# First down step of each expert chunk run one chunk later, with its weights loaded one chunk later

## The chip, the core and the metric

The kernel runs on one core of a Trainium2 chip. The metric is the device time of one execution in microseconds. Engines are named as the profile names them: PE is the matrix engine (its queue is PEq), DVE and ACT the vector and the scalar engine, POOL and SP the two others; SP issues nearly all transfers.

## The reference

A two-layer decoder trunk on 256 tokens of width 1024 in float32. What matters here is its last large part, a mixture of experts:

```python
logits = (xn @ router).astype(jnp.float32)
top_vals, top_idx = lax.top_k(logits, TOP_K)
...
for e in range(N_EXPERTS):
    out = out + combine[..., e:e + 1].astype(xn.dtype) * swiglu(xn, wg[e], wu[e], wd[e])
```

`swiglu` is `(silu(x @ wg) * (x @ wu)) @ wd`. There are 8 experts, each token goes to two of them, and the hidden width of an expert is 3584. All weights of all experts are read: 8 x 3 x 1024 x 3584 float32 numbers, 352 MB of the 447 MB that the program moves.

## The kernel before, in words

**Chunks.** The hidden width of an expert is cut into 7 chunks of 512 columns, so there are 56 chunks in `order`, numbered 0 to 55 here (chunks 0 to 6 are expert 0, 7 to 13 expert 1, and so on). A chunk has six weight tiles of 1 MB (128 x 2048 float32): two of gate, two of up, two of down.

**Slots.** The tokens of an expert are gathered into slots. The first 64 slots are always computed. Two further groups of 32 slots follow under `where_more`, which puts the work in a `tc.If` on the expert's count: more than 64 tokens opens group 0, more than 96 opens group 1 also. PE branches on that count.

**One pass of the loop (index i)** records, in this order:
1. `gate_up(i)`: 16 matmuls for the first 64 slots. The 64 output columns of the array's left half hold gate, those of the right half hold up, so two matmuls run side by side.
2. `hidden(i)`: silu and product on ACT and DVE. Then one piece of background work: a `gather` of the next expert's tokens (in an expert's last two chunks) or a `scatter` of a finished expert.
3. `where_more`: for the further groups, `down_b` of chunk i-2, transposes `turn_b` of chunk i-1, and `gate_up_b` of chunk i. `down_b` and `gate_up_b` use strips of 32 columns, so four matmuls run side by side.
4. `give_back`: the four gate and up tiles of chunk i and the two down tiles of chunk i-2 go back to the free list, and each is refilled at once by the next load of the stream (`Stream.load`, on SP, which waits until the tile's last reader is done).
5. `down` of chunk i-1 for the first 64 slots: 8 matmuls, `n` = 0 in the left half, `n` = 1 in the right half.
6. `turned_a(i)`: four transposes of the hidden values, copied by DVE to `hTa` for the next pass's `down`.

`with behind()` keeps the order of the first-slot steps on PE. What stands around them on an engine is set by the recording layer, not by the source alone.

**Loads.** The whole tiles are loaded in the order in which `add_whole` names them: gate and up of chunk i, then down of chunk i-1. There are 19 tile buffers in the pool at this stage. A down tile is read by `down` in one pass and by `down_b` in the next.

The functions and the loop follow, with the line numbers of the profile. In the profile of this kernel L1064 is `gate_up`, L1131 `down`, L1138 `down_b`, L1086 `gate_up_b`, L1113 the transposes of `turned_a`, L1121 those of `turn_b`, L994 `gather`, L1165 `scatter`, L1186 and L1189 the two branches of `where_more`, and L134 the loads on SP. One float32 matmul leaves two records.

Of the kernel before, what the change touches and what calls it, by code (L numbers as in the profile page):

```python
# [22 lines left out]
NT = T // P  # L23
# [13 lines left out]
NE, ED = 8, 3584  # L37
EC = ED // 512
# [178 lines left out]
def build(nc, tc, ctx, a, out):  # L217
# [15 lines left out]
    S = Stream(nc)  # L233

    def add_tiles(w, n):

        per, m = w.shape[2] // n, PS // n
        for t in range(w.shape[0]):
            S.add(w[t], [min(m, per - i) for i in range(0, per, m)], n)

    w = a["w_down_q"]
# [8 lines left out]
    t = 0  # L250
# [7 lines left out]
            add_tiles(a[w][g], 384)  # L258
    add_tiles(a["dsw_wo"], D)
    order = [(e, c) for e in range(NE) for c in range(EC)]  # L260
    for i, (e, c) in enumerate(order):
        if not i:
            add_tiles(a["moe_gate"][e, c], 512)
        for t in range(2):
            for nm in ("moe_gate", "moe_up")[not i:]:
                S.add_whole(a[nm][e, c][t])
        for t in range(2 if i else 0):
            S.add_whole(a["moe_down"][order[i - 1]][t])
    for t in range(2):
        S.add_whole(a["moe_down"][order[-1]][t])  # L270


    raw = pool(ctx, "raw", RAW)
# [43 lines left out]
    def bank(i, w=512):  # L317
        return psum.tile([P, 512], F32, name=f"b{i}", tag=f"b{i}")
# [6 lines left out]
    def split_to(hi, lo, src):  # L325
        return A.copy(hi, src), V.tensor_sub(lo, src, hi.bitcast(F32))
# [150 lines left out]
    bg = deque()  # L477

    def run(n=1):
        while bg and n > 0:  # L480
            bg.popleft()()
            n -= 1
# [209 lines left out]
    last = 5  # L692
# [163 lines left out]
    for g in range(8):  # L856
# [7 lines left out]
        for tt in range(NT):  # L864


            t, f = vs[g][:, tt], b[tt][:, :384].rearrange("p (b s d) -> p b s d", b=NBR, s=2)
# [182 lines left out]
    def group(g):  # L1050
        return slice(64 + 32 * g, 96 + 32 * g)
# [4 lines left out]
    def quadrant(g, i, part):  # L1056

        at = 64 * (g ^ part) + 32 * i
        return slice(at, at + 32)
# [50 lines left out]
    def turned_a(sg):  # L1110

        for j in range(4):
            x = PE.transpose(turns[:, j * 64:j * 64 + 64], sg[64:, j * P:(j + 1) * P], ident[64:, 64:])  # L1113
        t = mo.tile([P, 256], F32, name="hTa", bufs=2)
        V.tensor_copy(t, turns[:, :256])
        return t.rearrange("p (j s) -> p j s", j=4), x
# [6 lines left out]
    def turned_b():  # L1123
        t = mo.tile([P, 256], F32, name="hTb")
        A.copy(t, turns[:, 256:])  # L1125
        return t.rearrange("p (g j s) -> p g j s", g=2, j=4)

    def down(c, hT, y, w):
        for kt in range(4):
            for n in range(2):  # L1130
                x = PE.matmul(y[64 * n:64 * n + 64], hT[:, kt], w[n][:, kt * 512:(kt + 1) * 512],  # L1131
                              start=c + kt == 0, stop=c == EC - 1 and kt == 3)
        return x

    def down_b(c, g, hT, w):
        for kt in range(4):
            for n in range(2):
                PE.matmul(yB[g][quadrant(g, n, kt % 2)], hT[:, g, kt], w[n][:, kt * 512:(kt + 1) * 512],  # L1138
                          start=c == 0 and kt < 2, stop=c == EC - 1 and kt >= 2)

    def returned(y):
        f = gains.tile([P, D], F32, name="gain")
        for n, cols in enumerate(HALVES):
            (V.tensor_copy if n else A.copy)(f[:64, cols], y[64 * n:64 * n + 64])
        return f

    def returned_b(f):
        u = mo.tile([P, 512], F32, name="ub")
        for g in range(2):
            own = slice(64 * g, 64 * g + 64)  # L1150
            A.copy(u[own], yB[g][64 - 64 * g:128 - 64 * g])
            for n, cols in enumerate(HALVES):
                q = quadrant(g, n, 0)
                V.tensor_add(f[group(g), cols], yB[g][q], u[q])

    def scatter(e, f, n, tt, ye={}):

        cols = HALVES[n]
        if tt < 0:
            ye[0] = mo.tile([P, 2, 512], F32R, name="ye")  # L1160
            split_to(ye[0][:, 0], ye[0][:, 1], f[:, cols])
            return
        b = bank(1)
        for i in range(2):
            PE.matmul(b, ohT[e][:, tt * P:(tt + 1) * P], ye[0][:, i], start=i == 0, stop=i == 1)  # L1165
        x = h[:, tt, cols]
        V.scalar_tensor_tensor(x, b, comb[:, tt, e:e + 1], x, op0=OP.mult, op1=OP.add)  # L1167
        if e == NE - 1 and tt and not n:
            final_half(0)
# [3 lines left out]
    groups, w, held, sg_a, sg_b, hT_a, hT_b, y = {}, {}, {}, {}, {}, {}, {}, {}  # L1173

    def take(i, what, n):
        got = [S.take_whole() for _ in range(n)]
        held[i, what] = [j for j, _ in got]
        return [t for _, t in got]

    def give_back(i, what):  # L1180
        for j in held.pop((i, what)):
            S.give_back(j)
# [10 lines left out]
    def load_groups(e):  # L1193
        groups[e] = nc.tensor.value_load(more[0:1, e:e + 1], min_val=0, max_val=2)

    load_groups(0)
    n = len(order)
    last = None

    def behind():  # L1200
        return tc.issue_after(last.ins) if last else ExitStack()

    for i in range(n + 2):
        e, c = order[i] if i < n else (None, None)
        todo = {}
        if i >= 2:
            e2, c2 = order[i - 2]
            todo.setdefault(e2, []).append(lambda g, i=i, c2=c2: down_b(c2, g, hT_b[i - 2], w[i - 2, "down"]))
        if 1 <= i <= n:
            todo.setdefault(order[i - 1][0], []).append(lambda g, i=i: turn_b(g, sg_b[i - 1]))  # L1210
        if i < n:
            gu = bank(int(i == 1))
            if i:
                got = take(i, "gu", 4)
                ws = [(0, got[::2]), (1, got[1::2])]
            else:
                ws = [(1, take(i, "gu", 2))]
                for tt in range(NT):
                    PE.matmul(gu[:64], oh[:, tt, :64], gh[:, tt], start=tt == 0, stop=tt == NT - 1)

                def first_b(g):
                    for tt in range(NT):
                        PE.matmul(guB[g][quadrant(g, 0, tt)], oh[:, tt, group(g)], gh[:, tt], start=True, stop=True)
                todo[0] = [first_b]
            with behind():
                last = gate_up(e, gu, ws) if i else first_up(gu, ws[0][1])
            if i == 1:

                with behind():
                    hT_a[0], last = turned_a(sg_a.pop(0))  # L1230
            sg_a[i] = hidden(gu) if i else first_hidden(gu)
            todo.setdefault(e, []).append(lambda g, e=e, ws=ws: gate_up_b(e, g, ws))
            if i == 2:
                weights_of_experts()
            with behind():
                if e + 1 < NE and c >= EC - 2:
                    if c == EC - 2:
                        oh = slots(e + 1)
                    gather(e + 1, parts, oh, c - (EC - 2), bank(1))
                elif not c and e:  # L1240
                    slots_T(e, oh)
                else:
                    run(1)
        for e1, fs in todo.items():
            with behind():
                where_more(e1, fs)
        if i < n:
            give_back(i, "gu")
        if i >= 2:
            give_back(i - 2, "down")  # L1250
            if c2 == EC - 1:
                f = y.pop(e2)
                returned_b(f)
                bg.extend(lambda e2=e2, f=f, n=n, tt=tt: scatter(e2, f, n, tt) for n in range(2) for tt in range(-1, NT))
                if e2 == NE - 1:
                    run(99)
        if 1 <= i <= n:
            hT_b[i - 1] = turned_b()
            e1, c1 = order[i - 1]
            w[i - 1, "down"] = take(i - 1, "down", 2)  # L1260
            if c1 == 0:
                ya = bank(6)
            with behind():
                last = down(c1, hT_a.pop(i - 1), ya, w[i - 1, "down"])
            if c1 == EC - 1:
                y[e1] = returned(ya)
        if i < n:
            if i:
                with behind():
                    hT_a[i], last = turned_a(sg_a.pop(i))  # L1270
            sg_b[i] = hidden_b()
            if c == EC - 1 and e + 1 < NE:
                with behind():
                    load_groups(e + 1)
            with behind():
                run(1)
# [15 lines left out]
    for tt, r in enumerate(rs):  # L1292
        x, y = (fin["o"][:, tt, cols] for cols in HALVES)
# [68 lines left out]
```

## Time and profile before

| what | value |
|---|---|
| time, median of 3 runs | 1507.55 us (1502.9 to 1507.83) |
| profiled execution, its own time | 1501.57 us |
| its span, first to last instruction | 1499.7 us |
| granted PE clock, mean | 0.992 |
| busy: PE, DVE, ACT | 1434.0, 708.7, 616.6 us |
| moved by DMA | 447.38 MB |

The profile is of one execution, which was 6 us faster than the median of the three timed runs. Times in the profile run from its first instruction. The expert stage is the stretch from about 604 us to the end.

### The profile page before, as it was taken

Reading aid. Unit: us, or ns where it says so; the run is one execution under the profiler, and the core shown is the slowest. Engines: PE = TensorE matmul, PEld = TensorE weight load, DVE = VectorE, ACT = ScalarE, POOL = GpSimd, SP = SyncE. Lnnn points to the kernel's source line nnn. Section 1 sums busy time; section 2 is a strip of 40 time slices with the busy share of each in tenths; the row PEclk is TensorE's granted clock in tenths of the full one; section 3 lists DMA queues with packets and bytes.
Section 4 is the critical chain, followed back from the end, with each engine's and each line's share of the span. In section 5 each row is a group of like instructions: output and inputs, shape, how many; then the busy total and the mean of one; then the engine's idle time right before and its main releaser. Section 6 shows DMA issues by size and latency. Waiting matters only on the chain. (4 is left out here: it accounts for less than half of the span.)

```text
span 1499.7 us, 22281 instructions
## 1 busy us (share of the span) xinstructions
PE 1434.0 (96%) x9063; PEld 828.7 (55%) x9063; DVE 708.7 (47%) x1210; ACT 616.6 (41%) x1113; POOL 16.3 (1%) x22
## 2 busy tenths in 40 slices
PE   9999999999999999999999999999999999998984
PEld 7778998789999987333333333333333333333331
DVE  7876545497777776533322433121332243432423
ACT  7955444477777783523212332112221233322312
POOL 1000000000000000000000000000000000000001
PEclk9999999999999999999999999999999999999997
DMA  7435555354444468799999999876788999999992
GB/s 284 169 117 196 173 194 186 109 185 165 149 147 150 166 263 332 290 421 419 421 421 376 419 419 421 363 304 257 307 354 348 366 418 420 420 420 420 420 421 108
DMA packets 65954, 447.38 MB, mean 298 GB/s; under 512 B 7696, under 2 KB 8336, under 8 KB 17552
## 3 DMA queue, kind: packets, MB, share of 16 engines
q1 hardware_dynamic: 65520, 444.77, 75.1%
q8 instruction: 109, 1.79, 0.5%
q10 hardware_dynamic: 288, 0.52, 0.1%
q14 instruction: 37, 0.30, 0.1%
HBM read 444.22 MB, written 1.05 MB: 297 GB/s over the span
## 5 line engine op out<-in xcount | busy, mean ns | idle before, releaser
L149 DVE TENSOR_TENSOR w<-raw,w 128x768 fp32r<-128x768 f32 (+3 forms) x202 | 211.4, 1061 | 87.3 <-ACT w L148 87.0
L148 ACT CAST w<-raw 128x768 fp32r<-128x768 f32 (+3 forms) x202 | 181.7, 919 | 115.6 <-PE b L449 54.2
L1131 PE MATMUL b<-raw,hTa 128*64 128x512 f32 x896 | 211.9, 598 | 8.3 <-PEq L1186 4.6
L1064 PE MATMUL b<-raw,xgl 128*64 128x512 f32 x896 | 206.6, 596 | 9.3 <-DMA raw<-moe_up 9.2
L1125 ACT COPY hTb<-b 128x256 f32<-128x256 f32 x56 | 20.9, 373 | 445.7 <-PEq L1186 242.4
L1064 PE MATMUL b<-raw,xgh 128*64 128x512 f32 x864 | 196.0, 596 | 5.4 <-DMA raw<-moe_up 5.1
L1091 DVE TENSOR_TENSOR sg<-b,sg 64x512 f32<-64x512 f32 x55 | 38.2, 695 | 241.9 <-ACT sg L1090 241.1
L1131 PEld LDWEIGHTS b<-raw,hTa 128*64 128x64 f32 x896 | 66.2, 136 | 128.8 <-issue 113.3
L1064 PEld LDWEIGHTS b<-raw,xgl 128*64 128x64 f32 x896 | 65.1, 137 | 130.4 <-issue 108.5
L1064 PEld LDWEIGHTS b<-raw,xgh 128*64 128x64 f32 x864 | 62.3, 137 | 119.7 <-issue 106.7
L1098 DVE TENSOR_TENSOR msg<-b,ub 64x512 f32<-64x512 f32 x112 | 77.2, 689 | 40.7 <-ACT ub L1097 37.5
L1167 DVE SCALAR_TENSOR_TENSOR h<-b,comb,h 128x512 f32<-128x512 f32 x32 | 24.0, 751 | 146.4 <-PE b L1165 146.1
L1097 ACT COPY ub<-b 64x512 f32<-64x512 f32 x112 | 65.0, 580 | 65.4 <-PE b L1086 62.0
L447 PE MATMUL b<-x1l,w 128*128 128x256 f32 x288 | 81.7, 284 | 0.0
L1106 ACT ACTIVATE ub<-msg 32x512 f32<-32x512 f32 x112 | 70.3, 627 | 27.5 <-DVE msg L1098 21.9
L449 PE MATMUL b<-x1h,w 128*128 128x256 f32 x288 | 81.5, 283 | 0.0
L448 PE MATMUL b<-x1h,w 128*128 128x256 f32 x288 | 81.5, 283 | 0.0
L1086 PE MATMUL b<-raw,xgl 128*32 128x512 f32 x672 | 75.0, 594 | 2.3 <-PEq L1189 0.9
L447 PE MATMUL b<-raw,w 128*128 128x256 f32 x244 | 72.3, 296 | 0.0
L449 PE MATMUL b<-raw,w 128*128 128x256 f32 x244 | 69.6, 285 | 0.0
L448 PE MATMUL b<-raw,w 128*128 128x256 f32 x244 | 69.5, 285 | 0.0
L487 ACT COPY dsw<-b 32x512 f32<-32x512 f32 (+1 forms) x128 | 60.3, 471 | 11.6 <-PE b L449 9.8
(313 smaller groups left out, 2370.1 us busy)
## 6 DMA issues: line engine op xcount, KB each, us to landing
raw<-moe_gate SPq DMA_DIRECT2D x112, 1024.0 KB, 15.6
raw<-moe_up SPq DMA_DIRECT2D x112, 1024.0 KB, 17.7
raw<-moe_down SPq DMA_DIRECT2D x112, 1024.0 KB, 17.4
raw<-dsw_k SPq DMA_DIRECT2D x16, 768.0 KB, 4.4
raw<-dsw_q SPq DMA_DIRECT2D x16, 768.0 KB, 4.4
raw<-dsw_v SPq DMA_DIRECT2D x16, 768.0 KB, 4.1
raw<-ffn_gate SPq DMA_DIRECT2D x11, 1024.0 KB, 4.8
raw<-ffn_up SPq DMA_DIRECT2D x11, 1024.0 KB, 4.8
```

Source lines behind the costliest of these rows:

```text
L148: self.nc.scalar.copy(wh[:, :s], t[:, at:at + s])
L149: self.nc.vector.tensor_sub(wl[:, :s], t[:, at:at + s], wh[:, :s].bitcast(F32))
L447: PE.matmul(o, wh[:, i, cols], xl[:, c + i], start=first, stop=False)
L448: PE.matmul(o, wh[:, i, cols], xh[:, c + i], start=False, stop=False)
L449: PE.matmul(o, wl[:, i, cols], xh[:, c + i], start=False, stop=last)
L487: A.copy(o[r:r + 32], src[r ^ 32:(r ^ 32) + 32])
L1064: x = PE.matmul(gu[64 * i:64 * i + 64], xg[e][:, k, :64], rows(w, k), start=k == 0, stop=k == KD - 1)
L1086: PE.matmul(guB[g][quadrant(g, i, k % 2)], xg[e][:, k, group(g)], rows(w, k), start=k < 2, stop=k >= KD - 2)
L1097: A.copy(other[own], b[of])
L1098: V.tensor_add(o[own], b[own], other[own])
L1106: A.activation(u[up], t[gate], AF.Silu)
L1131: x = PE.matmul(y[64 * n:64 * n + 64], hT[:, kt], w[n][:, kt * 512:(kt + 1) * 512], start=c + kt == 0, stop=c == EC - 1 and kt == 3)
```

## The change

`down` of the first 64 slots of chunk i-2 now runs in pass i, in the same pass as `down_b` of that chunk, and it is recorded after `where_more`. In the stream of loads, the down tiles of chunk i-2 (not i-1) follow gate and up of chunk i. The down tiles are taken just ahead of `where_more`. They go back to the free list after `down`. At the end, the down step of chunk 53 is put ahead of the last `gate_up`, and the last two chunks keep the former distance. In passes 1 and 2 the transposes `turned_a` of the chunk before run right behind `gate_up`. What was copied out of the bank of an expert's result (`returned`) is now copied in one go with the further groups' part.

```diff
+    downs = [([], [i - 2] if i >= 2 else []) for i in range(n - 1)] + [([n - 3], [n - 2]), ([], [n - 1])]
...
     for i, (e, c) in enumerate(order):
+        for j in downs[i][0]:
+            add_down(j)
...
-        for t in range(2 if i else 0):
-            S.add_whole(a["moe_down"][order[i - 1]][t])
...
+        for j in downs[i][1]:
+            add_down(j)
...
+    def run_down(j):
+        nonlocal last
+        take_down(j)
+        e, c = order[j]
+        if c == 0:
+            y[e] = bank(6)
+        with behind():
+            last = down(c, hT_a.pop(j), y[e], w[j, "down"])
...
+            late_turn = i - 1 if i in (1, 2) else None
...
+        for j in downs[i][1] if i <= n else ():
+            take_down(j)
         for e1, fs in todo.items():
             with behind():
                 where_more(e1, fs)
         if i < n:
             give_back(i, "gu")
+        if 1 <= i <= n:
+            hT_b[i - 1] = turned_b()
+            for j in downs[i][1]:
+                run_down(j)
         if i >= 2:
             give_back(i - 2, "down")
...
-            w[i - 1, "down"] = take(i - 1, "down", 2)
-            if c1 == 0:
-                ya = bank(6)
-            with behind():
-                last = down(c1, hT_a.pop(i - 1), ya, w[i - 1, "down"])
```

The following rows are PE's instructions as the two programs hold them (line, operation, output and inputs, size and count). Line numbers of the changed kernel are ten higher: `gate_up` is L1074, `down` L1141, `down_b` L1148, `gate_up_b` L1096, `turned_a` L1123, `turn_b` L1131, `gather` L1004, and the branches are L1196 and L1199.

PE, chunk 34 (the last of expert 4, with a gather for expert 5), before: `gate_up`, the branch, the further groups, and then the gather.

```order
L1064 MATMUL b_10869<-raw,xgh 64x512 x16
L1186 COMPARE_AND_BRANCH
L1138 MATMUL b_6488<-raw,hTb 32x512 x8
L1121 MATMUL b_6490<-cst,msg 128x32 x4
L1189 COMPARE_AND_BRANCH
L1138 MATMUL b_6489<-raw,hTb 32x512 x8
L1121 MATMUL b_6490<-cst,ub 128x32 x4
L1086 MATMUL b_6487<-raw,xgh 32x512 x16
L1189 UNCONDITIONAL_BRANCH x2
L1086 MATMUL b_6486<-raw,xgh 32x512 x16
L1186 UNCONDITIONAL_BRANCH x2
L994 LDWEIGHTS xph
```

Behind these rows come the rest of the gather and the 8 matmuls of `down` in one row. Now the same place of the changed program, from the last row of the gather on.

```order
L1004 MATMUL b_10881<-oh,xr 128x128
L1141 MATMUL b_10439<-raw,hTa 64x512
L1196 COMPARE_AND_BRANCH
L1148 MATMUL b_6488<-raw,hTb 32x512 x8
L1131 MATMUL b_6490<-cst,msg 128x32 x4
L1199 COMPARE_AND_BRANCH
L1148 MATMUL b_6489<-raw,hTb 32x512 x8
L1131 MATMUL b_6490<-cst,ub 128x32 x4
L1096 MATMUL b_6487<-raw,xgh 32x512 x16
L1199 UNCONDITIONAL_BRANCH x2
L1096 MATMUL b_6486<-raw,xgh 32x512 x16
L1196 UNCONDITIONAL_BRANCH x2
```

The gather now stands between `gate_up` and the branch. Of `down`, one matmul (`n` = 0, left half) stands ahead of the branch, and the other seven follow behind the further groups, right behind the last row shown, as one row (`x7`). A single matmul of `down` stands ahead of a branch like this in passes 2 and 7 to 54; in passes 3 to 6 the eight are together. The skip path of the branch waits until the matmuls ahead of it, the single one included, have ended.

PE, passes 1 and 2, before: `gate_up(1)`, transposes, the branch of pass 1, then `down(0)`, transposes and `gate_up(2)`.

```order
L1064 MATMUL b_6576<-raw,xgh 64x512 x16
L1113 MATMUL b_6490<-cst,sg 128x64 x4
L1186 COMPARE_AND_BRANCH
L1121 MATMUL b_6490<-cst,msg 128x32 x4
L1189 COMPARE_AND_BRANCH
L1121 MATMUL b_6490<-cst,ub 128x32 x4
L1086 MATMUL b_6487<-raw,xgh 32x512 x16
L1189 UNCONDITIONAL_BRANCH x2
L1086 MATMUL b_6486<-raw,xgh 32x512 x16
L1186 UNCONDITIONAL_BRANCH x2
L1131 MATMUL b_6658<-raw,hTa 64x512 x8
L1113 MATMUL b_6490<-cst,sg 128x64 x4
```

The same place of the changed program, behind the transposes that follow `gate_up(1)`.

```order
L1074 MATMUL b_6672<-raw,xgh 64x512 x5
L1196 COMPARE_AND_BRANCH
L1131 MATMUL b_6490<-cst,msg 128x32 x4
L1199 COMPARE_AND_BRANCH
L1131 MATMUL b_6490<-cst,ub 128x32 x4
L1096 MATMUL b_6487<-raw,xgh 32x512 x16
L1199 UNCONDITIONAL_BRANCH x2
L1096 MATMUL b_6486<-raw,xgh 32x512 x16
L1196 UNCONDITIONAL_BRANCH x2
L1074 MATMUL b_6672<-raw,xgh 64x512 x11
L1123 MATMUL b_6490<-cst,sg 128x64 x4
L1141 MATMUL b_6778<-raw,hTa 64x512
```

`down(0)` is gone from pass 1, and `gate_up(2)` is cut into 5 and 11 matmuls around the branch of pass 1.

PE, chunk 35 (the first of expert 5), before: both branches stand behind `gate_up`, first that of expert 4 with `down_b` and `turn_b`, then that of expert 5 with `gate_up_b`.

```order
L1064 MATMUL b_11020<-raw,xgl 64x512 x16
L1186 COMPARE_AND_BRANCH
L1138 MATMUL b_6488<-raw,hTb 32x512 x8
L1121 MATMUL b_6490<-cst,msg 128x32 x4
L1189 COMPARE_AND_BRANCH
L1138 MATMUL b_6489<-raw,hTb 32x512 x8
L1121 MATMUL b_6490<-cst,ub 128x32 x4
L1189 UNCONDITIONAL_BRANCH x2
L1186 UNCONDITIONAL_BRANCH
L1186 COMPARE_AND_BRANCH
L1189 COMPARE_AND_BRANCH
L1086 MATMUL b_6487<-raw,xgl 32x512 x16
```

The same place of the changed program.

```order
L1074 MATMUL b_11012<-raw,xgl 64x512 x16
L1196 COMPARE_AND_BRANCH
L1199 COMPARE_AND_BRANCH
L1096 MATMUL b_6487<-raw,xgl 32x512 x16
L1199 UNCONDITIONAL_BRANCH x2
L1096 MATMUL b_6486<-raw,xgl 32x512 x16
L1196 UNCONDITIONAL_BRANCH x2
L993 LDWEIGHTS oh
L993 MATMUL b_11032<-identb,oh 128x128
...
L1141 MATMUL b_10439<-raw,hTa 64x512
L1196 COMPARE_AND_BRANCH
```

The branch of the new expert, with `gate_up_b`, comes first now. The branch of the expert before follows behind the single matmul.

## Rows read from the trace of the kernel before

**Rows 1.** The page: busy time of the engines, and slices of the span.

```profile
PE 1434.0 (96%) x9063; PEld 828.7 (55%) x9063; DVE 708.7 (47%) x1210; ACT 616.6 (41%) x1113; POOL 16.3 (1%) x22
...
PE   9999999999999999999999999999999999998984
...
DMA  7435555354444468799999999876788999999992
GB/s 284 169 117 196 173 194 186 109 185 165 149 147 150 166 263 332 290 421 419 421 421 376 419 419 421 363 304 257 307 354 348 366 418 420 420 420 420 420 421 108
```

**Rows 2.** Busy time by stretch of the expert stage.

```profile
core 0: us, PE busy (x) PEld busy (x) DVE busy (x) ACT busy (x) POOL busy (x), PEclk, DMA share, GB/s
604.00:960.00 356.00, 346.24 (x2014) 119.98 (x2012) 122.71 (x193) 101.05 (x179) 0.00 (x0) 1.00 0.98 402
960.00:1173.00 213.00, 211.96 (x1436) 70.67 (x1432) 49.02 (x76) 39.74 (x71) 0.00 (x0) 1.00 0.79 310
1173.00:1472.00 299.00, 276.43 (x1305) 100.04 (x1302) 108.41 (x168) 86.35 (x154) 0.00 (x0) 1.00 1.00 413
```

**Rows 3.** PE in order of time, chunks 33 and 34: start, us, instruction [idle before].

```profile
1151.09 3.64 PE L1086 MATMUL b<-raw,xgh 128*32 128x512 f32 x32
...
1160.08 7.09 PE L1064 MATMUL b<-raw,xgh 128*64 128x512 f32 x32
1167.10 1.92 PE L1138 MATMUL b<-raw,hTb 128*32 128x512 f32 x16
1168.95 0.43 PE L1121 MATMUL b<-cst,msg 32*128 32x32 f32 x4
1169.53 3.64 PE L1086 MATMUL b<-raw,xgh 128*32 128x512 f32 x32
1173.11 0.28 PE L994 MATMUL b<-oh,xph 128*128 128x128 bf16 x2
...
1174.55 3.65 PE L1131 MATMUL b<-raw,hTa 128*64 128x512 f32 x16
```

**Rows 4.** SP's loads in order of time, refilled by chunks 33 and 34.

```profile
1153.47 0.38 SPq L134 DMA_DIRECT2D raw<-moe_gate  x1
...
1156.15 15.66 SPq L134 DMA_DIRECT2D raw<-moe_down  x2
1171.92 1.83 SPq L134 DMA_DIRECT2D raw<-moe_gate  x1
...
1175.21 13.06 SPq L134 DMA_DIRECT2D raw<-moe_down  x2
```

**Rows 5.** PE in order of time, chunk 38 and the start of 39.

```profile
1219.08 7.09 PE L1064 MATMUL b<-raw,xgl 128*64 128x512 f32 x32
1226.48 3.65 PE L1131 MATMUL b<-raw,hTa 128*64 128x512 f32 x16 [0.31 <-DMA raw<-moe_gate]
...
1231.12 1.08 PE L1064 MATMUL b<-raw,xgl 128*64 128x512 f32 x4
```

**Rows 6.** PE in order of time, chunks 45 and 46, expert 6.

```profile
1304.73 4.51 PE L1064 MATMUL b<-raw,xgh 128*64 128x512 f32 x18
1310.04 3.65 PE L1064 MATMUL b<-raw,xgh 128*64 128x512 f32 x14 [0.81 <-DMA raw<-moe_up]
...
1319.64 4.50 PE L1064 MATMUL b<-raw,xgh 128*64 128x512 f32 x18
```

**Rows 7.** PE in order of time, chunks 1 and 2.

```profile
616.06 0.46 PE L1113 MATMUL b<-cst,sg 64*128 64x64 f32 x4
619.36 3.65 PE L1131 MATMUL b<-raw,hTa 128*64 128x512 f32 x16 [2.84 <-DVE hTa L1115]
622.95 0.46 PE L1113 MATMUL b<-cst,sg 64*128 64x64 f32 x4
623.34 7.09 PE L1064 MATMUL b<-raw,xgh 128*64 128x512 f32 x32
630.73 3.65 PE L1131 MATMUL b<-raw,hTa 128*64 128x512 f32 x16 [0.31 <-PEq L1186]
```

**Rows 8.** PE in order of time, chunk 7, the first of expert 1.

```profile
690.97 3.64 PE L1086 MATMUL b<-raw,xgl 128*32 128x512 f32 x32 [0.92 <-PEq L1189]
```

**Rows 9.** PE in order of time, the last chunk and the tail.

```profile
1461.96 3.65 PE L1064 MATMUL b<-raw,xgl 128*64 128x512 f32 x14 [1.31 <-DMA raw<-moe_up]
...
1471.49 4.12 PE L1131 MATMUL b<-raw,hTa 128*64 128x512 f32 x16 [0.52 <-DVE hTa L1115]
...
1479.92 1.60 PE L1165 MATMUL b<-ye,ohT 128*128 128x512 f32 x2 [4.31 <-ACT ye L326]
```

More of the change, by code (lines that the diff above doesn't have):

```diff
@@ L260, in build, with add_down @@
     order = [(e, c) for e in range(NE) for c in range(EC)]
+    n = len(order)
+    downs = [([], [i - 2] if i >= 2 else []) for i in range(n - 1)] + [([n - 3], [n - 2]), ([], [n - 1])]
+    def add_down(j):
+        for t in range(2):
+            S.add_whole(a["moe_down"][order[j]][t])
     for i, (e, c) in enumerate(order):
+        for j in downs[i][0]:
+            add_down(j)
         if not i:
@@ L266, in build @@
                 S.add_whole(a[nm][e, c][t])
-        for t in range(2 if i else 0):
-            S.add_whole(a["moe_down"][order[i - 1]][t])
-    for t in range(2):
-        S.add_whole(a["moe_down"][order[-1]][t])
+        for j in downs[i][1]:
+            add_down(j)
+    for j in downs[-1][1]:
+        add_down(j)
     raw = pool(ctx, "raw", RAW)
@@ L1201, in behind, with take_down, return_of @@
         return tc.issue_after(last.ins) if last else ExitStack()
+    def take_down(j):
+        if (j, "down") not in w:
+            w[j, "down"] = take(j, "down", 2)
+    def run_down(j):
[6 more added lines that the diff above has]
+            last = down(c, hT_a.pop(j), y[e], w[j, "down"])
+    def return_of(e):
+        f = returned(y.pop(e))
+        returned_b(f)
+        bg.extend(lambda n=n, tt=tt: scatter(e, f, n, tt) for n in range(2) for tt in range(-1, NT))
     for i in range(n + 2):
         e, c = order[i] if i < n else (None, None)
+        for j in downs[i][0] if i <= n else ():
+            run_down(j)
         todo = {}
@@ L1226, in build @@
                 last = gate_up(e, gu, ws) if i else first_up(gu, ws[0][1])
-            if i == 1:
+            if late_turn is not None:
                 with behind():
-                    hT_a[0], last = turned_a(sg_a.pop(0))
+                    hT_a[late_turn], last = turned_a(sg_a.pop(late_turn))
             sg_a[i] = hidden(gu) if i else first_hidden(gu)
@@ L1248, in build @@
             give_back(i, "gu")
+        if 1 <= i <= n:
+            hT_b[i - 1] = turned_b()
+            for j in downs[i][1]:
+                run_down(j)
         if i >= 2:
             give_back(i - 2, "down")
[L1251 to L1259, printed above, removed]
-            w[i - 1, "down"] = take(i - 1, "down", 2)
-            if c1 == 0:
-                ya = bank(6)
-            with behind():
-                last = down(c1, hT_a.pop(i - 1), ya, w[i - 1, "down"])
-            if c1 == EC - 1:
-                y[e1] = returned(ya)
+        if i >= 2 and c2 == EC - 1:
+            return_of(e2)
+            if i > n:
+                run(99)
         if i < n:
-            if i:
+            if i > 1:
                 with behind():
```

## Prediction

> **What bounds the kernel now.** The page comes first. PE is busy for 96% of the span and its row of slices is full nearly to the end, while the DMA row reaches 9 only in two stretches [rows 1]. So the next view is busy time by stretch of the expert stage [rows 2]. From 604 to 960 us both are nearly full: PE 346.24 of 356 us, DMA share 0.98. From 960 to 1173 us PE has 211.96 of 213.00 us and DMA 0.79: PE sets the pace, the loads wait for buffers. From 1173 to 1472 us the DMA share is 1.00 at 413 GB/s and PE has only 276.43 of 299 us: the loads set the pace.
>
> The place where one takes over from the other is in chunk 34, and the loads show it. SP issues a load when a tile comes free. The tiles that chunk 33 gives back are refilled from 1153.47 us on, and SP then stands in the issue of the next pair until 1171.81 (1156.15 + 15.66); the tiles that chunk 34 gives back are refilled from 1171.92 us on [rows 4]. That is the end of `gate_up_b` of chunk 34 on PE (1169.53 to 1173.17, [rows 3]; the first tiles are read out a little before its end). From there 116 tiles follow without a gap, 299 us, and then some 28 us of tail: the last `down` at 1471.49 us waits 0.52 us for `hTa`, and the last scatter waits for `ye` [rows 9]. So **the time ends at a fixed distance behind the give-back of chunk 34.** Whatever delays PE up to there delays the end one to one. What PE does later counts only if PE can't catch up with the loads.
>
> **The change, part by part.** I sum the shift of that give-back, in us, against the profiled execution's own 1501.57 us (span 1499.7 us). The median is 1507.55, 6 us above it.
>
> *What is loaded when.* Each give-back still refills six tiles, and in the new stream the tile that stands last before the gate tiles of a chunk is only another down pair. The number of loads that are out at each give-back of gate and up is unchanged. The down pair itself comes back behind `down` and no longer ahead of it, 3.65 us later [rows 3]. SP takes these in line, so the loads queued behind the pair would wait too; but in the stretch up to 1173 us loads wait for PE anyway, and from there they are one backlog. I take 0, with up to 3.65 us as the upper bound, once.
>
> *Start of the stage.* `down(0)` in pass 1 waits 2.84 us for `hTa`, which DVE has just copied, and then takes 3.65 us [rows 7]. Both go: `gate_up(2)` covers the copy, and what is moved from a chunk ahead of the give-back to one behind it counts once, −3.65 − 2.84 = −6.5. Against that, `gate_up(2)` is cut into 5 and 11 matmuls around a branch. Its 16 take 7.09 us as 8 rounds of two side by side [rows 7], so 0.89 us for a round; 5 and 11 take 3 + 6 = 9 rounds, +0.9, and a branch behind matmuls opens a gap of 0.31 us [rows 7]. Sum −5.3.
>
> *The single matmul ahead of the branch.* This is the large term, and only the order shows it. `down`'s 8 matmuls take 3.65 us because left and right half run side by side: 4 rounds [rows 3]. In the changed program one matmul of the left half stands ahead of the branch. Behind it come, on PE's queue, either the further groups, which use all four strips, or the skip path, which waits until that matmul has ended. So its half of the array is in use and the other idle. The nearest rows are pieces of `gate_up` that a load cut at an odd place: 18 records (9 matmuls) take 4.51 and 4.50 us and 14 records (7 matmuls) take 3.65 us [rows 6], like the 16 of `down` (3.65). So the ninth matmul costs 4.51 − 3.65 = 0.86 us, and taking one away from eight saves nothing: the other half still has four. A chunk pays 0.86 us. Up to chunk 34 such singles stand in chunks 2 and 7 to 34, 29 of them: 29 x 0.86 = **+24.9**. Bounds: 0 if the single runs beside what stands next to it; 1.2 us each (34 in all) if the branch's gap of 0.31 us is paid a second time [rows 5, 7].
>
> Here a rule of the Trainium skill bears on the trace. In chunk 34, `gate_up` with 64-column halves ends at 1160.08 + 7.09 = 1167.17 us, and `down_b` with 32-column strips starts at 1167.10 us [rows 3]: no idle time at the switch. The Trainium skill, "TensorEngine Tiling (Array Packing)", section Key Properties, says that a change of the tiling mode drains TensorE. By that rule the single matmul of a 64-column half can't lie beside the 32-column strips of the further groups, which is what the sum has; by the row alone an overlap of some hundredths of a us at either side is allowed, and the sum would be the same within 1 us.
>
> *First chunks of an expert.* The new expert's branch now comes first. In chunk 7 two branches in a row cost 0.92 us ahead of `gate_up_b` [rows 8]; with one of them behind the give-back some 0.4 us are left. The same place is in chunks 14 and 21: three times −0.52 = −1.6, by estimate; 0 if the gap stays.
>
> *Gather.* In an expert's last two chunks the gather's 12 matmuls stood behind the further groups and now stand ahead of the branch. They lie on PE either way. Only for chunk 34, whose give-back now stands behind them, do they count: 1174.55 − 1173.11 = +1.4 [rows 3].
>
> Sum: −5.3 + 24.9 − 1.6 + 1.4 = **+19.4 us**, 1521.0 us on the profile's own time, and 1527 us from the median. I take **1523**.
>
> *Behind chunk 34.* Another 20 singles follow (35 to 54). A load-bound chunk needs six tiles, 15.0 us at 420 GB/s (6 x 1.0486 MB; [rows 1]), and shows it: `gate_up` of chunk 45 starts at 1304.73, that of 46 at 1319.64 us, 14.9 us apart, with waits for `moe_up` [rows 6]. Unstarved chunks take 12.0 us (1219.08 to 1231.12, [rows 5]), 12.9 with a single. So PE still gains 2 us a chunk on the loads and waits again before the last chunk. These singles cost nothing, and the order of the last two chunks is as before, so the tail stays.
>
> **Rivals.** *The singles cost nothing*, the other side. If the other half's matmuls behind the branch start beside the single, or if the single fills a hole that the branch leaves anyway (0.31 us, [rows 5, 7]), only the other terms are left: −5.3 − 1.6 + 1.4 = −5.5, so 1496 us on the profile's own time and 1502 from the median. For it speaks that PE's records are pipelined and starts overlap ends in [rows 3]. Against it: the skip path waits for the single's end, and the ninth matmul in [rows 6] did cost a full 0.86 us. It decides where a single costs under 0.2 us (29 x 0.2 = 5.8).
>
> *Half price.* The single takes the room of the gap behind `gate_up` in chunks without further groups, and its full price in the others: about 0.43 us on average, 29 x 0.43 = 12.5, less 5.5: +7, so 1508.6 to 1514.
>
> *Dearer.* Each single also opens a second branch gap (29 x 0.31 = +9.0), or the down pair returned late holds up the gates of a chunk in the load-bound part (+3.65): 1525 to 1536. The same comes out if PE doesn't catch up behind chunk 34; that takes a cost per chunk of some 1.6 us above the forecast's.
>
> *The change doesn't do what it says*: `down` and `down_b` of a chunk do stand in one pass now and each down tile is read in one pass, but no more loads are out at a give-back than before, so nothing is gained by it; this is contained in all cases.
>
> **How the numbers follow.** About 0.5%, 7.5 us, is what a measurement of this kernel can tell from no change. Forecast (1515 to 1528) 0.68, singles for nothing (1496 to 1502) 0.13, half price (1506 to 1514) 0.08, dearer (1525 to 1536) 0.11. Slower by over 0.5% (above 1515.1): the forecast and the dearer case, and a little of the half price, 0.80. Singles for nothing lie within 0.5% from 1500.0 on, and half price too: same 0.15, faster 0.05. The range leaves out the free singles and the far end of the dearer case: 1506 to 1533. The likeliest case's own range is 1515 to 1528.
>
> **What the changed kernel's profile would show.** In PE's order of time, right behind each `gate_up` a piece of `down` with 2 records and, behind the branch, one with 14 records that still takes 3.65 us. Chunks 21 to 34 0.86 us longer each. The wait of 2.84 us near 619 us gone. The loads of chunk 34's tiles issued at about 1191 instead of 1171.92 us, and the stretch of full DMA ending near 1491 us. Waits of PE for `moe_up` return only late in expert 7, but before the last `gate_up`. The prediction is wrong if the two pieces of `down` together take 3.65 us, if the loads have another gap later than chunk 34, or if PE reaches its last chunk without having waited for a load.

## The result, and the profile after

The changed kernel takes 1524.72 us (median of 4 runs, 1521.93 to 1525.08) against 1507.47 us before: a ratio of 1.0117, interval 1.0099 to 1.0136, so 17 us slower. The forecast was 1523.

First the page of the changed kernel: busy times, and the slices of PE and DMA.

```profile
PE 1470.7 (97%) x9063; PEld 835.1 (55%) x9063; DVE 708.8 (47%) x1210; ACT 617.1 (41%) x1113; POOL 16.3 (1%) x22
...
PE   9999999999999999999999999999999999999984
...
DMA  7435555354444477799998999575877899999992
```

PE has as many instructions as before and is busy 36.7 us longer (1434.0 in [rows 1]). The DMA row falls to 5 in the stretch where it stood at 6 to 8 before: the loads wait for buffers longer. The busy time by stretch; the borders behind 604 us are moved to the same places of the program, so the first stretch also holds what was lost ahead of the expert stage (2.8 us, below):

```profile
core 0: us, PE busy (x) PEld busy (x) DVE busy (x) ACT busy (x) POOL busy (x), PEclk, DMA share, GB/s
604.00:973.00 369.00, 364.44 (x2025) 126.22 (x2025) 123.29 (x194) 102.22 (x181) 0.00 (x0) 1.00 0.95 392
973.00:1197.00 224.00, 222.79 (x1456) 74.00 (x1456) 49.03 (x76) 40.38 (x72) 0.00 (x0) 1.00 0.72 293
1197.00:1495.00 298.00, 283.35 (x1296) 96.79 (x1288) 108.37 (x168) 85.64 (x152) 0.00 (x0) 1.00 1.00 415
```

Against [rows 2], the first stretch is 13 us longer (369 to 356), the second 11 us (224 to 213), and the third is as long as before (298 to 299). The time was lost while PE sets the pace, and none where the loads do. Chunk 34 in PE's order of time, beside [rows 3] (the gather of this pass stands between the first two rows):

```profile
1182.25 7.09 PE L1074 MATMUL b<-raw,xgh 128*64 128x512 f32 x32
...
1190.71 1.07 PE L1141 MATMUL b<-raw,hTa 128*64 128x512 f32 x2
1191.71 1.92 PE L1148 MATMUL b<-raw,hTb 128*32 128x512 f32 x16
...
1194.15 3.64 PE L1096 MATMUL b<-raw,xgh 128*32 128x512 f32 x32
1197.72 3.65 PE L1141 MATMUL b<-raw,hTa 128*64 128x512 f32 x14
```

`down` is two pieces. The single matmul (2 records) keeps PE from 1190.71 to 1191.71 us, 1.00 us, and the other seven (14 records) still take the 3.65 us of eight. A chunk without further groups, beside [rows 5]:

```profile
1244.59 7.09 PE L1074 MATMUL b<-raw,xgl 128*64 128x512 f32 x32
1251.51 1.02 PE L1141 MATMUL b<-raw,hTa 128*64 128x512 f32 x2
1252.68 3.62 PE L1141 MATMUL b<-raw,hTa 128*64 128x512 f32 x14 [0.15 <-PEq L1196]
```

Here the gap at the branch is 0.15 us and no longer 0.31. SP's loads around the give-back of chunk 34:

```profile
1181.95 0.33 SPq L134 DMA_DIRECT2D raw<-moe_gate  x1
1196.11 0.33 SPq L134 DMA_DIRECT2D raw<-moe_up  x1
```

The give-back is refilled from 1196.11 us, 24 us later than the 1171.92 of [rows 4]. Of these, 2.8 us had been lost ahead of the expert stage (below). The tail is the old one: the last `down` starts at 1495.09 us, 28.2 us ahead of the span's end at 1523.3 us; before it was 1499.7 − 1471.49 = 28.2 us [rows 9].

The start of the stage, beside [rows 7]:

```profile
619.22 2.79 PE L1074 MATMUL b<-raw,xgh 128*64 128x512 f32 x10
622.15 5.33 PE L1074 MATMUL b<-raw,xgh 128*64 128x512 f32 x22
...
627.81 1.07 PE L1141 MATMUL b<-raw,hTa 128*64 128x512 f32 x2
629.03 3.62 PE L1141 MATMUL b<-raw,hTa 128*64 128x512 f32 x14 [0.15 <-PEq L1196]
```

The wait of 2.84 us for `hTa` is gone, and `gate_up(2)` is cut in two pieces that take 8.26 us together with the branch between them (7.09 whole).

### The profile page after: what moved, and what is told of

It is laid out like the page before. It is cut to its first block, busy times and chain, and to the rows that moved or that the text cites. A ratio compares the mean times of both kernels' runs of the same rounds, so it can differ in the third digit from the quotient of the medians.

```text
span 1523.3 us, 22284 instructions
## 1 busy us (share of the span) xinstructions
PE 1470.7 (97%) x9063; PEld 835.1 (55%) x9063; DVE 708.8 (47%) x1210; ACT 617.1 (41%) x1113; POOL 16.3 (1%) x22
## 5 line engine op out<-in xcount | busy, mean ns | idle before, releaser
L1141 PE MATMUL b<-raw,hTa 128*64 128x512 f32 x896 | 257.9, 600 | 9.2 <-PEq L1196 3.1
L1074 PE MATMUL b<-raw,xgl 128*64 128x512 f32 x896 | 204.2, 596 | 7.4 <-DMA raw<-moe_up 7.4
L1074 PE MATMUL b<-raw,xgh 128*64 128x512 f32 x864 | 192.4, 595 | 0.4 <-PEq L1196 0.3
L1100 ACT ACTIVATE sg<-b 64x512 f32<-64x512 f32 x55 | 32.4, 588 | 361.7 <-PE b L1074 340.0
L1141 PEld LDWEIGHTS b<-raw,hTa 128*64 128x64 f32 x896 | 74.0, 136 | 161.4 <-issue 144.5
L1074 PEld LDWEIGHTS b<-raw,xgl 128*64 128x64 f32 x896 | 63.8, 137 | 127.0 <-issue 110.6
L1074 PEld LDWEIGHTS b<-raw,xgh 128*64 128x64 f32 x864 | 60.5, 137 | 113.0 <-issue 111.4
L1135 ACT COPY hTb<-b 128x256 f32<-128x256 f32 x56 | 20.8, 372 | 160.0 <-PEq L1196 79.0
L1096 PE MATMUL b<-raw,xgl 128*32 128x512 f32 x672 | 75.0, 594 | 1.1 <-PEq L1199 0.2
```

What stands on the lines that cost most here:

```text
L1074: x = PE.matmul(gu[64 * i:64 * i + 64], xg[e][:, k, :64], rows(w, k), start=k == 0, stop=k == KD - 1)
L1096: PE.matmul(guB[g][quadrant(g, i, k % 2)], xg[e][:, k, group(g)], rows(w, k), start=k < 2, stop=k >= KD - 2)
```

## The experiments

Three theories. **A**: the time is the half of the array that is idle beside the single matmul, and it counts up to the give-back of chunk 34. **B**: a cut of `down` around a branch has a price, whatever piece of it stands ahead. **C**: the time comes from the later loads of the down tiles or from the moved gather, not from the single.

One table serves all of them. It is worked out from the first row of `gate_up` of chunks 1, 3 and 35 in PE's order of time of each trace, and from the span's end; all times are in us.

| kernel | chunk 1 starts | 1 to 3 | 3 to 35 | 35 to end |
|---|---|---|---|---|
| before | 609.04 | 25.66 | 543.82 | 321.2 |
| before, second trace | 611.64 | 27.37 | 543.82 | 321.2 |
| changed | 611.81 | 21.16 | 568.72 | 321.6 |
| eight behind | 608.72 | 20.19 | 542.39 | 320.8 |
| pair ahead | 611.64 | 20.39 | 547.41 | 324.3 |
| two of the left half ahead | 612.26 | 22.03 | 600.08 | 328.1 |
| single put into before | 612.68 | 29.06 | 573.12 | 323.7 |
| singles only behind chunk 34 | 608.99 | 20.20 | 542.42 | 321.5 |
| old stream of loads | 612.52 | 20.20 | 542.58 | 321.3 |
| early turn | 613.59 | 25.43 | 542.31 | 321.9 |
| whole `gate_up(2)`, gather behind | 611.51 | 19.38 | 542.51 | 320.2 |

**Eight behind.** `down` is queued behind all branches of its pass (`fences` holds the last instruction that each `where_more` recorded, and `behind_all` opens an `issue_after` for each).

```diff
             for j in downs[i][1]:
-                run_down(j)
+                with behind_all(fences):
+                    run_down(j)
```

> The changed kernel with all 8 matmuls of down behind the branches; nothing else moves on PE. Theory A (the single matmul leaves half of the array idle): the 29 singles up to chunk 34 go, 27 us by the measured steps of 0.65 to 1.0 us a chunk, so 1498 us, ratio to before about 0.994. Theory B (each cut of down around a branch has a price, whatever stands ahead of it): the same, since the cut goes too. Theory C (the later loads of the down tiles or the gather ahead of the branch cost the time): stays at 1520 to 1525 us.

Measured: 1498.46 us, ratio to before 0.995 (0.9933 to 0.9967). Chunk 34:

```profile
1152.86 7.09 PE L1074 MATMUL b<-raw,xgh 128*64 128x512 f32 x32
...
1161.32 1.92 PE L1148 MATMUL b<-raw,hTb 128*32 128x512 f32 x16
...
1163.76 3.64 PE L1096 MATMUL b<-raw,xgh 128*32 128x512 f32 x32
1167.33 3.65 PE L1141 MATMUL b<-raw,hTa 128*64 128x512 f32 x16
```

The 26 us are back, so C falls: later loads, moved gather and moved step are all still in this kernel, and it is even 0.5% faster than before. Between A and B this run can't tell, since the cut goes with the single. From chunk 3 to 35 it needs 568.72 − 542.39 = 26.3 us less than the changed kernel, for 28 singles: 0.94 us each.

**Pair ahead, two of the left half ahead.** `down` takes a list of steps; those of `AHEAD` are recorded ahead of the branches, the rest behind them, as in eight behind. The first kernel's `AHEAD` is shown; in the second it is `[(0, 0), (1, 0)]`. In the kernels with such a list `down` is L1143 and `down_b` L1150.

```diff
+    AHEAD = [(0, 0), (0, 1)]
...
         for j in downs[i][1] if i <= n else ():
-            take_down(j)
+            run_down(j, AHEAD)
...
-                run_down(j)
+                with behind_all(fences):
+                    run_down(j, [s for s in STEPS if s not in AHEAD])
```

> The changed kernel with one matmul of each half (a pair) ahead of the branches in every pass from 2 on, six behind. Theory A: one full round ahead and three behind, no idle half; only a branch gap of about 0.15 us in chunks without further groups is left, 1498 to 1503 us. Theory B: 33 cuts up to chunk 34 at 0.93 us, 1528 us.

> The changed kernel with two matmuls of the left half ahead of the branches in every pass from 2 on; behind them two of the left and four of the right. Theory A: two half-idle rounds a chunk, 33 x 1.86 = 61 us above the kernel with eight behind, 1559 us, and up to 1570 if PE then no longer catches up with the loads. Theory B: one cut a chunk, 33 x 0.93, 1528 us.

Measured: 1505.84 us with the pair (ratio 1.0004, 0.9994 to 1.0014), 1564.16 us with two of the left half (1.0391, 1.037 to 1.0411). Chunk 34 with the pair:

```profile
1169.31 1.08 PE L1143 MATMUL b<-raw,hTa 128*64 128x512 f32 x4
1170.32 1.92 PE L1150 MATMUL b<-raw,hTb 128*32 128x512 f32 x16
...
1176.32 2.79 PE L1143 MATMUL b<-raw,hTa 128*64 128x512 f32 x12
```

And with two of the left half:

```profile
1222.54 1.93 PE L1143 MATMUL b<-raw,hTa 128*64 128x512 f32 x4
1224.40 1.92 PE L1150 MATMUL b<-raw,hTb 128*32 128x512 f32 x16
...
1230.40 3.65 PE L1143 MATMUL b<-raw,hTa 128*64 128x512 f32 x12
```

These four rows of `down` decide between A and B. Both kernels put two matmuls ahead and six behind, with the same cut. As a pair the two take 1.08 us and the six 2.79, 3.87 together where eight take 3.65. From one half the two take 1.93 us and the six still 3.65, 5.58 together. From chunk 3 to 35, 32 chunks, the pair costs 547.41 − 542.39 = 5.0 us over eight behind, 0.16 us a chunk, and the two of one half 57.7 us, 1.80 us a chunk: nearly twice the single's 0.94. So B falls as the main cause: the cut itself costs 0.16 us, and the rest of the single's price, some 0.78 us, is the idle half. The pair's time is 3 us above the range expected under A: it needs 3.5 us more than eight behind from chunk 35 to the end, and why stays open. With two of one half PE doesn't catch up with the loads any more: 328.1 us from chunk 35 to the end, where 321 is usual, and no wait of `gate_up` for a load is left.

The Trainium skill, "TensorEngine Tiling (Array Packing)", section Key Properties, says that a change of the tiling mode drains TensorE. In chunk 34 the pair puts a 64-column piece between the gather and the 32-column strips, and the chunk takes 18.59 us where it takes 18.44 with eight behind (from its first row of `gate_up` to that of chunk 35); the cost of a drain, if there is one here, lies within these 0.15 us.

**Single put into before.** The kernel before, with only the first matmul of `down` recorded ahead of its branches.

```diff
+            with behind():
+                last = down(c1, hT_a[i - 1], ya, w[i - 1, "down"], AHEAD)
+        fences = []
...
-            with behind():
-                last = down(c1, hT_a.pop(i - 1), ya, w[i - 1, "down"])
+            with behind(), behind_all(fences):
+                last = down(c1, hT_a.pop(i - 1), ya, w[i - 1, "down"], [s for s in STEPS if s not in AHEAD])
```

> The kernel before, with nothing changed but that one matmul of down stands ahead of the branches in every pass from 1 on (loads, tiles and the chunk that down works on as before). Theories A and B: 34 singles up to chunk 34 at 0.93 us, 1507.5 + 32 = 1539 us. Theory C: 1507 us, since the loads are those of before.

Measured: 1541.32 us, ratio 1.0239 (1.0219 to 1.0258). From chunk 3 to 35 it is 573.12 − 543.82 = 29.3 us over before, 0.92 us for each of 32 singles. The price belongs to the single, in either kernel.

**Singles only behind chunk 34.** Eight behind, with a single ahead in passes 35 to 54 (the edit is shown against eight behind).

```diff
-            take_down(j)
+            if 35 <= i <= 54:
+                run_down(j, AHEAD)
+            else:
+                take_down(j)
...
-                    run_down(j)
+                    run_down(j, STEPS[1:] if 35 <= i <= 54 else STEPS)
```

> The kernel with eight behind (measured 1498.5 us), with a single of down ahead of the branches again in passes 35 to 54 alone, 20 of them. Theory A (a delay of PE counts only up to the give-back of chunk 34, from where the loads are the bound): 1498 us, unchanged, and PE's waits for moe_up begin some chunks later. Rival D (a single costs its 0.93 us wherever it stands): 1498.5 + 18.6 = 1517 us.

Measured: 1499.09 us, ratio 0.9954 (0.9938 to 0.9969), the same as eight behind. The singles stand in the trace, 1.02 us here:

```profile
1306.45 7.09 PE L1074 MATMUL b<-raw,xgh 128*64 128x512 f32 x32
1313.37 1.02 PE L1143 MATMUL b<-raw,hTa 128*64 128x512 f32 x2
1314.54 3.62 PE L1143 MATMUL b<-raw,hTa 128*64 128x512 f32 x14
```

This `gate_up` of chunk 45 starts 10 us later than with eight behind (1296.48), and that of chunk 55 only half a microsecond later (1447.98 to 1447.44): the loads have taken over in between. So what a single costs behind chunk 34 doesn't reach the end, as forecast, and rival D falls.

**Old stream of loads.** Eight behind, the down tiles of chunk i-1 loaded behind gate and up of chunk i again. PE's order was held by further `issue_after`, apart from single transposes.

```diff
-        for j in downs[i][1]:
-            add_down(j)
+        if i:
+            add_down(i - 1)
...
                 got = take(i, "gu", 4)
+                take_down(i - 1)
```

> The kernel with eight behind, with the stream of loads of the kernel before (gate and up of a chunk, then down of the chunk ahead of it by one, not two); PE's order stays. Theory A (the number of tiles loaded at each give-back is the same either way, so the later loads by themselves are worth nothing): 1498 us, within 2. Rival E (the gain of the kernel with eight behind comes from the gate and up tiles that now arrive two loads earlier): back by up to two loads, 5 us, to 1503.

Measured: 1496.97 us, ratio 0.9933 (0.9918 to 0.9948); each stretch of the table is within 0.5 us of eight behind. So rival E falls, and the weights loaded later are worth nothing by themselves.

**Early turn; whole `gate_up(2)` with the gather behind.**

```diff
-            late_turn = i - 1 if i in (1, 2) else None
+            late_turn = 0 if i == 1 else None
```

> The kernel with eight behind, with the transposes of chunk 1 at the end of pass 1 again, as in the kernel before, so that gate_up of chunk 2 is whole. The round of 0.9 us and the gap that the cut costs go (-1.2), the wait of PE for the hidden values of chunk 1 comes back (0 to 2.8 us): 1497 to 1500 us; in the trace gate_up of chunk 3 starts 1.2 us earlier to 1.6 us later than with eight behind, seen from gate_up of chunk 1.

```diff
-            with behind():
+            with behind(), behind_all(fences if i == 2 else []):
                 last = gate_up(e, gu, ws) if i else first_up(gu, ws[0][1])
...
-                    gather(e + 1, parts, oh, c - (EC - 2), bank(1))
...
+        if i < n and e + 1 < NE and c >= EC - 2:
+            with behind_all(fences):
+                gather(e + 1, parts, oh, c - (EC - 2), bank(1))
```

> The kernel with eight behind, with gate_up of chunk 2 whole behind the branch of pass 1 (-0.9 us), and with each gather behind the branches of its pass, so that the give-back of chunk 34 doesn't wait for it (-1.4 us): 1496 us, ratio to before 0.993 to 0.994. If the gather delays nothing there: 1497.5.

Measured: 1503.82 us for the early turn (0.9979, 0.997 to 0.9988), 4 us more than expected, and 1494.31 us for the other (0.9917, 0.9903 to 0.993), the fastest kernel of the study. In the early turn PE's transposes wait for the hidden values, and the clock falls. PE's order of time there, and then the windows with the granted clock (third figure from the right):

```profile
624.72 0.66 PE L1123 MATMUL b<-cst,sg 64*128 64x64 f32 x4 [3.66 <-DVE sg L1101]
625.31 9.57 PE L1074 MATMUL b<-raw,xgh 128*64 128x512 f32 x32
```

```profile
613.00:621.00 8.00, 7.70 (x37) 2.97 (x36) 5.79 (x9) 7.34 (x12) 0.00 (x0) 1.00 0.67 264
...
626.00:628.00 2.00, 2.00 (x8) 0.55 (x6) 1.91 (x4) 1.42 (x3) 0.00 (x0) 0.50 1.02 430
...
632.00:634.00 2.00, 2.00 (x12) 0.70 (x10) 0.00 (x0) 0.00 (x0) 0.00 (x0) 1.00 0.34 139
```

The wait was 3.66 us, beyond the 2.8 allowed for, and behind it the clock was granted at 0.50 (1.2 GHz), so `gate_up(2)` took 9.57 us and not 7.09. That is 3.66 + 2.48 us, less the 1.2 of the cut. Against eight behind, the other kernel gains 0.8 us from chunk 1 to 3 (forecast 0.9) and 0.6 us from chunk 35 to the end (forecast 1.4). That makes 1.3 us with the 0.1 lost in between, while the medians are 4 us apart. The medians also hold the start of the stage, which moves from one execution to the next (608.72 to 613.59 us in the table); how much of the rest that is stays open.

SP's loads show what the moved gather does. Eight behind first, then the kernel with the gather behind:

```profile
1165.72 0.33 SPq L134 DMA_DIRECT2D raw<-moe_up  x1
...
1171.43 0.40 SPq L134 DMA_DIRECT2D raw<-moe_gate  x1
```

```profile
1166.36 0.33 SPq L134 DMA_DIRECT2D raw<-moe_up  x1
...
1173.52 0.45 SPq L134 DMA_DIRECT2D raw<-moe_gate  x1
```

The first of the six loads that chunk 34 lets go is issued 7.04 us ahead of `gate_up` of chunk 35 (1173.40) with the gather behind, and 5.58 ahead (of 1171.30) without: 1.46 us earlier, the forecast's 1.4. The last of the six is issued 0.1 us behind that start in both, after `down`.

**Both kernels once more.**

> The kernel before once more, for a second trace. In the traces so far gate_up of chunk 1 starts near 609 us or near 612 us, with the same program ahead of it. If that is chance of an execution and not of a kernel, this one starts at either; an execution of 1507 us should then start late, near 612, and lose the other 3 us at some place between there and the give-back of chunk 34.

> As the run ahead of it: gate_up of chunk 1 near 609 or near 612 us; the distance from the end of the last idle time of the loads to the end is 325 to 328 us, as in all traces so far.

> The changed kernel once more. From gate_up of chunk 1 to gate_up of chunk 35 it needs 589.9 us, within 1, wherever it starts; the kernel before needed 569.5 us for the same stretch.

Measured: 1505.9, 1506.63 and 1525.21 us. The changed kernel needs 589.8 us from chunk 1 to 35, as expected (589.9 in the first trace). The kernel before starts at 611.64 and 612.55 us this time, and needs 27.37 us from chunk 1 to 3 in both, 1.7 more than in the first trace. The place is `down(0)`, behind its wait for `hTa`:

```profile
621.97 5.35 PE L1131 MATMUL b<-raw,hTa 128*64 128x512 f32 x16 [2.85 <-DVE hTa L1115]
```

The wait is the same as in [rows 7], and the 16 records take 5.35 us and not 3.65. From 624 to 626 us the granted clock was 0.58, a mean over a stretch with both levels, where the first trace shows 1.00. The second trace and then the first:

```profile
624.00:626.00 2.00, 2.00 (x8) 0.63 (x6) 1.91 (x4) 1.48 (x3) 0.00 (x0) 0.58 1.03 434
```

```profile
623.00:627.00 4.00, 4.00 (x24) 1.61 (x24) 1.73 (x3) 0.00 (x0) 0.00 (x0) 1.00 1.01 426
```

The 3 us ahead of the stage go with a low clock too:

```profile
580.00:590.00 10.00, 8.39 (x38) 6.81 (x37) 7.28 (x14) 3.24 (x7) 1.40 (x1) 0.74 0.82 322
```

In the first trace of before these ten microseconds have the same busy time and a clock of 1.00, with 52 instructions begun where here there are 38.

## Why the prediction was right

**The bound.** Right in the main. PE sets the pace up to the give-back of chunk 34, and the end lies at a nearly fixed distance behind. From SP's first refill behind chunk 34 to the end it is 327.7 to 327.8 us in the three traces of before, 327.2 and 327.4 in the two of changed, and 326.4 to 329.0 in all others but the one with two of the left half ahead (333.7). From chunk 35 to the end it is 320.2 to 324.3 us in the same kernels. Two details of the prediction fail. The loads of before do not run without a gap from there on. They have a second, smaller hole in chunk 35:

```profile
1187.00:1188.00 1.00, 0.82 (x12) 0.32 (x4) 0.00 (x0) 0.05 (x1) 0.00 (x0) 1.00 0.80 336
1188.00:1189.00 1.00, 0.22 (x4) 0.15 (x4) 0.00 (x0) 0.91 (x2) 0.00 (x0) 1.00 0.45 98
1189.00:1190.00 1.00, 1.00 (x7) 0.43 (x8) 0.88 (x3) 0.89 (x2) 0.00 (x0) 1.00 0.56 139
```

That is 1.2 us of DMA time; the changed kernel has no such hole there. And PE doesn't need 1.6 us a chunk above the forecast's cost to stay behind the loads to the end: two of the left half cost 1.80 in all, 0.94 above the forecast's 0.86, and there it already does. In the changed kernel PE still waits seven times for `moe_up`, first at 1419.48 us in chunk 51, so it has caught up there, as forecast.

**The singles.** Right in place and cause, and too small by a tenth: forecast 0.86 us each and +24.9 in all, measured 0.97 in pass 2 and 26.3 for the other 28, so +27.3. The term was mis-sized in two parts: the cut's own price, 0.16 us by the pair, stood at nothing, since the rows of `gate_up` [rows 6] couldn't show it, and the idle half by itself came to some 0.78 us and not 0.86.

**The start.** Forecast −5.3, measured without the single 20.19 − 25.66 = −5.5 against the profiled execution. Against the second trace of before it is −7.2, since there the wait also brought the low clock.

**First chunks of an expert.** Forecast −1.6; with eight behind chunks 7, 14 and 21 take 0.55, 0.16 and 0.31 us less than before, −1.0 in all: the −0.52 read from chunk 7 held there and not in the two others. From chunk 3 to 35 eight behind gains 1.4 us over before; a part of the rest is the branch gaps of 0.31 us that are now 0.15, which I had not foreseen.

**The gather.** Forecast +1.4, measured some +0.4 us from chunk 35 to the end. The give-back itself moves by the forecast's amount, as the run with the gather behind shows (1.46 us). Why it reaches the end only in part wasn't tried by itself; two things in the traces may do it, that the last of the six loads is issued behind `down`, which the gather doesn't delay against chunk 35, and that the hole of before in chunk 35 is gone.

The sum was +19.4. From chunk 1 on it is −5.5 + 27.3 − 1.4 + 0.4 = +20.8 us against the profiled execution and +19.1 against the second trace. The medians differ by 17.3. The forecast of 1523 was 1.7 us low: the singles cost more than forecast, and the wait that the change removes costs more too in executions with the lower clock, as two of the three traces of before show. That the number came so near is in part luck: 1523 was picked between 1521, the sum on the profile's time, and 1527, the sum on the median, and the misses of the singles (+2.4) and of the gather (−1.0) partly cancel.

Of the rivals, singles for nothing and half price are excluded by eight behind. The dearer case falls too: a single costs 0.94 us and not 1.17, a chunk without further groups has one branch gap of 0.15 us with a single and none of 0.31, and from chunk 35 to the end the changed kernel takes 0.4 us more than before, not 3.65. That the change gains nothing by its loads was right for the loads (old stream), and wrong for the whole: without the single the whole change is worth 0.5%, from the start of the stage above all.

## What to carry to other kernels

Look at the order that the recording layer makes of a moved step, not only at the source: one instruction of eight on the wrong side of a branch turned a gain of 0.5% into a loss of 1.2%. Where halves of the array work side by side, cut a step between pairs. And find the place where the bound changes hands: here a single cost 0.94 us ahead of that place, and 20 of them behind it cost nothing that the medians show.

## What the runs showed of the hardware that was not expected

In this kernel a wait of PE can cost more than itself: behind idle times of 2.85 and 3.66 us the granted clock was 0.58 and 0.50 for some microseconds in the rows above, and the work behind took 1.7 and 2.5 us longer; after a wait of 2.84 us in another execution it stayed at 1.00. So one program gives spans of 1499.7 and 1504.0 us with the same wait there: of the 4.3 us, 2.6 were lost ahead of the stage and 1.7 behind this wait. Why the clock fell in one execution and not in the other, no run here shows.
